# A two-layer decoder trunk on one core: the high part of x's first piece in two operations, and the squares for its row sums begun behind the second piece

## Chip, core and metric

The kernel runs on one core of a Trainium2 chip. The metric is the device time of one execution in microseconds (us); the median of several runs is given, with the lowest and the highest.

## What is computed

Two layers, each a row norm, one wide projection, four head groups and an output projection that is added to x. Cut to what the change touches:

```python
def rmsnorm(x, g):
    y = x * lax.rsqrt(jnp.mean(x * x, axis=-1, keepdims=True) + EPS)
    return y * g

def hybrid_layer(x, positions, norm_g, w_in, ..., w_out):      # x: (1, 512, 1024) float32
    h = rmsnorm(x, norm_g)
    p = h @ w_in                                               # (1024, 3488)
    (cq, ckv, kr, g_a, c_h, c_b, c_c, g_b, sg_u, sg_v, g_c, mq, mk, mv, g_d) = jnp.split(p, offs, axis=-1)
    q = rmsnorm(cq, mla_q_norm_g) @ mla_w_uq                   # low-rank q and kv
    kv = rmsnorm(ckv, mla_kv_norm_g) @ mla_w_ukv
    # (A) latent attention, (B) gated short convolution, (C) spatial gating, (D) block-sparse attention
    ...
    return jnp.concatenate([o_a * silu(g_a), o_b * silu(g_b), o_c * silu(g_c), o_d * silu(g_d)]) @ w_out

for l in range(2):
    x = x + hybrid_layer(x, ...)
```

## The kernel before

**Split products.** TensorE (PE) takes the operands of the products in the type fp32r. To keep more of float32 than that, every operand is split into a high part, the value rounded, and a low part, the rest, and every product is made of three: high by high, high by low, low by high. The high parts are written by ScalarE (ACT) or VectorE (DVE), the low parts by DVE, which reads the high part and the source. In the names h or hi stands for a high part and l or lo for a low one: hTh and hTl are the parts of x transposed, whi_ and wlo_ those of a weight unit, cTh and cTl those of cq and ckv transposed, yTh and yTl those of the first three sq units (they are kept in a buffer that later holds the heads' outputs).

**The start of layer 0.** x is (512 tokens, 1024). It arrives as pieces of 128 columns: piece k, 0 to 7, is transposed on PE into one PSUM bank (the tile xT, 128 columns of x by 512 tokens, `x_transpose`), then `x_parts` writes its high part on ACT, with the norm's gain as the scale, and its low part on DVE. Layer 0 does not divide by the row norm before the product. It multiplies by the unnormed x and puts the factor in later, so the product can start before the row sums are known. `c_first` makes the first products, cq (416 columns, in four blocks of 128 tokens): for each of the first six pieces the order on PE is four products of the high parts, the four transposes of the next piece, four with the weight's low part, four with x's low part. The weights of this product come as four units c0 to c3, each with two pieces' rows; c0's two halves land one after the other.

**The row sums.** `x_stats` squares x on ACT, 16 operations of 128 x 256 (four token blocks in each of four pairs of pieces, tile junk with the sums in xsum), each with an accumulator that is read after it. When a pair is done and transposed, its slot (one of four, x_0 .. in the rows) is released and serves others, the raw data of the units sq2 and sq3 among them, which the SP queue loads in a fixed order (`load_units`). When all are done, DVE adds the sums (TENSOR_REDUCE xv and three small TENSOR_SCALAR xv) and sets the event `v_ev`. The norms of cq and ckv (`low_stats`: ssq, e, ms) wait for it, since the factor left out changes their epsilon; ms is raised to the power -0.5 on GpSimd (POOL), and then scales the values Vt and the rotary key krt. POOL makes the rotary tables (rope_scratch) in the same stretch.

**After cq.** `low_chain` copies each token block of cq (ct), transposes it (cT), splits it (cTh, cTl) and makes q and kv from it with the units uq and ukv; the products of the token weights sq, for the spatial gate and the block-sparse queries, are interleaved.

**What sets the order.** Nothing is scheduled by hand. The class `Order` holds a clock for PE (`now`) and one for each other engine, and a list of generators with priorities. Each generator, a `Chain`, issues an instruction when its own time `t` is no more than 300 ns ahead of `now`; the clocks go forward by cost formulas in `Chain.act`, `dve`, `pool` and `pe`. An engine executes its instructions in the order in which they were issued in this way. A weight unit's high part goes to ACT or to DVE by which of the two clocks is behind (`split_units`), so an operation that is issued elsewhere can change the engine of another, and the order of all that follows. While PE has nothing to do in the first 15 us, filler products (tile warm) are issued.

Lines: all operations that go through a `Chain` have line 179 on ACT, DVE and POOL and line 209 on PE; most DMA issues of the SP queue have line 296. `x_parts` begins at line 760, `x_stats` at line 773.

Of the kernel before, what the change touches and what calls it, by code (L numbers as in the profile page):

```python
# [14 lines left out]
AF = mybir.ActivationFunctionType  # L15
# [3 lines left out]
P = 128  # L19
S = 512  # L20
# [201 lines left out]
def hybrid_trunk(ctx: ExitStack, tc: tile.TileContext, x, positions, norm_g, w_c, w_f, w_t, w_o, mla_q_norm_g,  # L222
# [3 lines left out]
    V, A, G, PE = nc.vector, nc.scalar, nc.gpsimd, nc.tensor  # L226
# [16 lines left out]
    o = Order()  # L243
# [479 lines left out]
    def pow_rstd(ch, dst, src, n):  # L723
        return ch.pow(G.tensor_tensor, dst, src, nhalf[:, :n], op=ALU.pow)
# [5 lines left out]
    xhi, xlo = ([Event() for _ in range(KT)] for _ in range(2))  # L730
# [18 lines left out]
    def x_transpose(k):  # L749

        ch = Chain(o)
        tp = yield from trS.get(ch, f"xT{k}")
        yield from ch.wait(xk_ev[k])
        for t in range(NT):
            yield from ch.pe(109.0, PE.transpose, tp[:, t * P:(t + 1) * P],
                             xk[k // 2][:, t, (k % 2) * P:(k % 2 + 1) * P], ident)
        o.set(xk_tr[k], ch.t)
        o.spawn(x_parts(k, tp, ch.t), None, -8)

    def x_parts(k, tp, t0):  # L760
        L, ch = layers[0], Chain(o, t0)
        if k // 4 not in L.h:
            L.h[k // 4] = [big.tile([P, 4, S], F32R, tag=f"h{x}{k // 4}", name=f"hT{x}{k // 4}_0") for x in "hl"]
        hi, lo = hk(L, k)
        g = gcol[:, k:k + 1]
        yield from ch.act(A.activation, hi, tp, AF.Copy, scale=g)
        o.set(xhi[k], ch.t)
        yield from ch.dve(V.scalar_tensor_tensor, lo, in0=tp, scalar=g, in1=hi.bitcast(F32),
                          op0=ALU.mult, op1=ALU.subtract)
        o.set(xlo[k], ch.t)  # L770
        trS.put(ch)

    def x_stats():
        ch = Chain(o)
        for kp in range(KT // 2):
            yield from ch.wait(xk_ev[2 * kp + 1])
            for t in range(NT):
                yield from ch.act(A.activation, junk[:, 0:2 * P], xk[kp][:, t, :], AF.Square, scale=D ** -0.5,
                                  accum_out=xsum[:, t, kp:kp + 1])
            c2 = Chain(o, ch.t)  # L780
            yield from c2.wait(xk_tr[2 * kp + 1])
            v4S.put(c2)
        yield from ch.dve(V.tensor_reduce, xv[:, RV, :], xsum, axis=AX.X, op=ALU.add)
        yield from ch.dve(V.tensor_scalar, xv[:, RV, :], xv[:, RV, :], 1.0, EPS, op0=ALU.mult, op1=ALU.add)
        t0 = ch.t
        for i, f in ((RE, EPS), (REE, EPS * EPS)):
            yield from ch.dve(V.tensor_scalar, xv[:, i, :], xv[:, RV, :], f, None, op0=ALU.mult)
        o.set(v_ev, ch.t)
        c2 = Chain(o, max(t0, ROWT))
        yield from pow_rstd(c2, xv[:, RR, :], xv[:, RV, :], NT)  # L790

        yield from c2.dve(V.tensor_copy, xr2[:, 0, :], xv[:, RR, :])
        yield from c2.dve(V.tensor_tensor, xr2[:, 1, :], xv[:, RR, :], xr2[:, 0, :].bitcast(F32), op=ALU.subtract)
        o.set(r_ev, c2.t)
# [118 lines left out]
    def hk(L, k):  # L913
        hi, lo = L.h[k // 4]
        return hi[:, k % 4, :], lo[:, k % 4, :]
# [1152 lines left out]
    def start():  # L2068
# [38 lines left out]
        o.spawn(split_units(4, len(order)), None, 5)  # L2107
        o.spawn(rope_tables(), 3700.0, 4)
        o.spawn(x_stats(), None, 5)
        o.spawn(x_row(), ROWT, 5)  # L2110
        o.spawn(main(), None, 10)
# [53 lines left out]
```

## Time and profile before

| | |
|---|---|
| three runs | 485.35, 485.96 and 486.68 us; median 485.96 |
| the profiled execution | 485.9 us, its span in the profile 484.2 us |
| granted clock of TensorE | 1.00 of full speed |
| instructions | 7554 |
| DMA | 94.21 MB in 41760 packets, mean 195 GB/s |

The profile is one execution. Times in it count from the start of its span; a row of a timeline has start, duration, engine, line, operation, the tile written, the tiles read, shapes, and in brackets how long the engine had been idle before and what released it. PEld is TensorE's loading of the stationary operand, which runs beside its products. An ACT operation's row is longer than the distance to the next one's start, since they overlap; an operation with an accumulator is followed by a row that reads it.

### The profile page before, as it was taken

To read this page: it belongs to the slowest core of one execution; us is meant where nothing else is said; L and a number is where in the kernel's file an instruction comes from. 1 tells how busy PE (TensorE), PEld (TensorE's weight loads), DVE (VectorE), ACT (ScalarE), POOL (GpSimd) and SP (SyncE) were. 2 spreads that over 40 slices of the span, in tenths; PEclk is the share of its full clock that TensorE was granted. 3 is DMA by queue.
4 is the path that set the end of the run, shared out by engine and by line. 5 is a ranking of instruction groups with operands and counts; after the bars stand their busy time and mean duration, and the time that the engine had idled before them with its cause. 6 is when DMAs were issued, how large, how long until landed. Compare 5 with 4: busy or idle time off the path is not lost. (4 is left out here: it accounts for less than half of the span.)

```text
span 484.2 us, 7554 instructions
## 1 busy us (share of the span) xinstructions
PE 478.2 (99%) x2418; PEld 406.6 (84%) x2418; DVE 399.4 (82%) x883; ACT 335.0 (69%) x895; POOL 115.2 (24%) x187
## 2 busy tenths in 40 slices
PE   8999999999999999999999999999999999999996
PEld 7988888888888888888899888888888888888785
DVE  3698877978798997779898679997788998888992
ACT  5897757776568674457577788788686888676640
POOL 8858713310421052000031004262102200000000
PEclk9999999999999999999999999999999999999999
DMA  8823076996698798685663277987824852248762
GB/s 265 306 87 110 12 229 242 235 232 168 184 282 190 219 270 260 233 283 178 214 238 131 86 268 244 263 176 226 185 87 144 161 156 106 104 158 276 271 216 87
DMA packets 41760, 94.21 MB, mean 195 GB/s; under 512 B 6114, under 2 KB 22328, under 8 KB 41336
## 3 DMA queue, kind: packets, MB, share of 16 engines
q1 hardware_dynamic: 28400, 80.74, 48.2%
q0 software_dynamic: 13216, 12.91, 17.6%
q8 instruction: 19, 0.31, 0.3%
q14 instruction: 21, 0.17, 0.1%
q10 hardware_dynamic: 104, 0.07, 0.1%
HBM read 85.58 MB, written 33.29 MB: 246 GB/s over the span
## 5 line engine op out<-in xcount | busy, mean ns | idle before, releaser
L179 ACT ACTIVATE pd<-pd,mnd 128x128 f32<-128x128 f32 (+3 forms) x53 | 27.2, 541 | 3.7 <-DVE mnd L179 3.5
L179 ACT ACTIVATE pa<-pa,mna 128x128 f32<-128x128 f32 (+3 forms) x55 | 28.1, 539 | 1.8 <-DVE mna L179 1.6
L375 POOL DMA_DIRECT2D t<-in_w_o_dram x16 | 18.6, 1323 | 30.5 <-DMA t<-t 30.4
L179 ACT ACTIVATE pha<-pTa 128x512 fp32r<-128x512 f32 (+3 forms) x32 | 13.8, 436 | 15.1 <-PE pTa L209 14.5
L179 ACT ACTIVATE phd<-pTd 128x512 fp32r<-128x512 f32 (+3 forms) x32 | 13.7, 433 | 13.0 <-PE pTd L209 12.8
L209 PE MATMUL cq<-whi_c,hTh 128*128 128x416 f32 x64 | 20.6, 367 | 0.4 <-ACT hTh L179 0.3
L179 DVE TENSOR_TENSOR pla<-pTa,pha 128x512 fp32r<-128x512 f32 (+3 forms) x32 | 15.1, 485 | 7.1 <-ACT pha L179 7.0
L179 ACT ACTIVATE whi_t<-raw_t 128x512 fp32r<-128x512 f32 x32 | 18.5, 618 | 3.3 <-DMA raw_t<-t 3.3
L179 DVE CUSTOM_DVE_ANT_0 pa<-sa,maskb,rs_q 128x512 f32<-128x512 f32 (+3 forms) x32 | 16.6, 545 | 4.8 <-PE pTa L209 2.7
L179 DVE TENSOR_TENSOR wlo_t<-raw_t,whi_t 128x512 fp32r<-128x512 f32 x32 | 20.6, 680 | 0.0
L209 PE MATMUL cq<-wlo_c,hTh 128*128 128x416 f32 x64 | 20.0, 358 | 0.0
L209 PE MATMUL cq<-whi_c,hTl 128*128 128x416 f32 x64 | 19.8, 356 | 0.0
L179 DVE TENSOR_TENSOR wlo_p<-raw_p,whi_p 128x512 fp32r<-128x512 f32 x28 | 18.9, 698 | 0.7 <-ACT whi_p L179 0.6
L179 DVE TENSOR_TENSOR pld<-pTd,phd 128x512 fp32r<-128x512 f32 (+3 forms) x32 | 15.1, 486 | 4.6 <-ACT phd L179 4.3
L179 DVE CUSTOM_DVE_ANT_0 pd<-sd,maskb,rs_mq 128x512 f32<-128x512 f32 (+3 forms) x32 | 16.7, 545 | 1.6 <-PE pTd L209 0.8
L179 ACT ACTIVATE whi_b<-raw_b 128x512 fp32r<-128x512 f32 x23 | 13.8, 621 | 4.1 <-DMA raw_b<-in_w_o_dram 4.0
L179 DVE TENSOR_TENSOR wlo_b<-raw_b,whi_b 128x512 fp32r<-128x512 f32 x24 | 16.1, 683 | 0.1
L179 ACT ACTIVATE whi_p<-raw_p 128x512 fp32r<-128x512 f32 x26 | 15.6, 625 | 0.7 <-DMA raw_p<-p 0.7
L179 POOL TENSOR_TENSOR rs_mk<-rs_mk,nhalf 128x16 f32<-128x16 f32 x2 | 5.9, 2926 | 42.5 <-ACT gc L179 21.5
L179 POOL TENSOR_SCALAR xss<-xss 128x1 f32<-128x1 f32 x4 | 2.7, 669 | 54.6 <-ACT jk L179 50.2
L375 POOL DMA_DIRECT2D p<-in_w_t_dram x8 | 9.8, 1486 | 23.0 <-DMA p<-p 11.8
L209 PE MATMUL pTa<-ident,pa 128*128 128x128 f32 x80 | 14.0, 273 | 0.0
(499 smaller groups left out, 1854.4 us busy)
## 6 DMA issues: line engine op xcount, KB each, us to landing
t<-in_w_o_dram POOLq DMA_DIRECT2D x16, 512.0 KB, 8.6
raw_t<-t SPq DMA_DIRECT2D x16, 512.0 KB, 4.9
raw_b<-in_w_o_dram SPq DMA_DIRECT2D x12, 512.0 KB, 5.0
t<-in_w_o_dram SPq DMA_DIRECT2D x8, 512.0 KB, 5.3
p<-in_w_t_dram POOLq DMA_DIRECT2D x8, 512.0 KB, 12.4
t<-t SPq DMA_DIRECT2D x8, 512.0 KB, 4.9
raw_p<-p SPq DMA_DIRECT2D x8, 512.0 KB, 4.7
ys<-ysc SPq DMA_DIRECT2D x14, 256.0 KB, 5.6
```

Source lines behind the costliest of these rows:

```text
L179: f(*a, **k)
L209: f(*a, **k)
L375: nc.gpsimd.dma_start(src(l, n, j), src(l, y, j), accum_op=ALU.add, max_dma_last_dim=1024)
```

## The change

The high part of piece 0 is written by two ACT operations, of tokens 0 to 255 and 256 to 511, and the planner's event for it is set by the first of them. The other seven pieces are left as they were. The chain that issues the squares starts with the time 8600 ns where it started with the planner's clock at that moment, so its first square is issued later among ACT's instructions.

```diff
         g = gcol[:, k:k + 1]
-        yield from ch.act(A.activation, hi, tp, AF.Copy, scale=g)
-        o.set(xhi[k], ch.t)
+        n = 2 * P if k == 0 else S
+        yield from ch.act(A.activation, hi[:, 0:n], tp[:, 0:n], AF.Copy, scale=g)
+        t1 = ch.t
+        if n < S:
+            yield from ch.act(A.activation, hi[:, n:S], tp[:, n:S], AF.Copy, scale=g)
+        o.set(xhi[k], t1)
         yield from ch.dve(V.scalar_tensor_tensor, lo, in0=tp, scalar=g, in1=hi.bitcast(F32),
                           op0=ALU.mult, op1=ALU.subtract)
         o.set(xlo[k], ch.t)
         trS.put(ch)
 
     def x_stats():
-        ch = Chain(o)
+        ch = Chain(o, 8600.0)
         for kp in range(KT // 2):
             yield from ch.wait(xk_ev[2 * kp + 1])
             for t in range(NT):
```

The number of squares, of products for the result and of bytes moved stays as it is. Since the order of everything behind these two places is worked out anew by the planner, it differs on all engines in layer 0; PE's differs up to its row 916 of 2271 in the program's order, and is the same from there on. One filler product at the start is gone, and two of the high part's operations stand where one stood.

## The prediction

> **What bounds the kernel now.** I read the profile from the whole to the place: first the page's busy times, then TensorE's (PE's) busy time by stretches of the span, then the waits of PE, then the timelines of the first 30 us, engine by engine. The page's first part, and two stretches and the sum from the table of busy time by windows (length, then busy time of PE, PEld, DVE, ACT and POOL, then granted clock, DMA share and GB/s):
>
> ```profile
> PE 478.2 (99%) x2418; PEld 406.6 (84%) x2418; DVE 399.4 (82%) x883; ACT 335.0 (69%) x895; POOL 115.2 (24%) x187
> ...
> 0.00:5.70 5.70, 4.16 (x21) 3.68 (x21) 1.44 (x5) 2.15 (x3) 3.84 (x44) 1.00 0.62 166
> 5.70:20.00 14.30, 14.12 (x81) 12.99 (x81) 8.44 (x14) 12.02 (x39) 12.48 (x30) 1.00 1.04 376
> 20.00:40.00 20.00, 20.00 (x107) 17.74 (x107) 18.29 (x47) 18.03 (x62) 13.40 (x23) 1.00 0.29 84
> ...
> 460.00:484.20 24.20, 20.32 (x101) 17.09 (x99) 15.34 (x27) 5.19 (x10) 0.00 (x0) 1.00 0.45 151
> sum 484.20, PE 478.17 PEld 406.57 DVE 399.36 ACT 335.01 POOL 115.15; mean PE 36.78 PEld 31.27 DVE 30.72 ACT 25.77 POOL 8.86
> ```
>
> PE is idle for 484.20 - 478.17 = 6.0 us in all: 5.70 - 4.16 = 1.5 us before its first real product, 0.2 us in the next 14, 24.20 - 20.32 = 3.9 us behind its last work, and 0.4 us in the 440 us between. So PE's in-order stream sets the time. An edit gains only what it takes from the idle time at the start, and loses whatever it makes PE wait later. In the same 20 us that follow the start, DVE (18.29 of 20.00) and ACT (18.03) are nearly full as well: work that is pushed into that stretch has little cover. PE's timeline at the start (start, duration, instructions of four each; a merged row's duration includes the tail of its last product):
>
> ```profile
> 5.77 1.02 PE L209 MATMUL cq<-whi_c,hTh 128*128 128x416 f32 x4 [0.33 <-ACT hTh L179]
> ...
> 7.82 0.92 PE L209 MATMUL cq<-whi_c,hTl 128*128 128x416 f32 x4
> 8.84 1.02 PE L209 MATMUL cq<-whi_c,hTh 128*128 128x416 f32 x4
> ...
> 10.89 0.92 PE L209 MATMUL cq<-whi_c,hTl 128*128 128x416 f32 x4
> 11.65 0.99 PE L209 MATMUL cq<-whi_c,hTh 128*128 128x416 f32 x4
> ...
> 29.25 0.45 PE L209 MATMUL q<-whi_uq,cTl 128*128 128x384 f32 x1
> ```
>
> Four products without a wait take 11.65 - 10.89 = 0.76 us. PE was therefore free for piece 1 at 7.82 + 0.76 = 8.58 and began at 8.84: 0.26 us of waiting that the page's tails hide. ACT's timeline beside it:
>
> ```profile
> 5.03 0.69 ACT L179 ACTIVATE hTh<-xT,pg 128x512 fp32r<-128x512 f32 x1 [1.81 <-PE xT L209]
> ...
> 7.26 0.55 ACT L179 ACTIVATE whi_c<-raw_c 128x416 fp32r<-128x416 f32 x1 [0.94 <-DMA raw_c<-in_w_c_dram]
> 7.72 0.40 ACT L179 ACTIVATE junk<-x 128x256 f32<-128x256 f32 x1
> ...
> 8.12 0.67 ACT L179 ACTIVATE hTh<-xT,pg 128x512 fp32r<-128x512 f32 x1
> ...
> 10.04 0.55 ACT L179 ACTIVATE whi_c<-raw_c 128x416 fp32r<-128x416 f32 x1 [0.31 <-DMA raw_c<-in_w_c_dram]
> 10.49 0.40 ACT L179 ACTIVATE junk<-x 128x256 f32<-128x256 f32 x1
> ...
> 10.89 0.67 ACT L179 ACTIVATE hTh<-xT,pg 128x512 fp32r<-128x512 f32 x1
> ...
> 32.18 0.48 ACT L179 ACTIVATE Q<-q 128x384 f32<-128x384 f32 x1
> ...
> 33.21 0.36 ACT L179 ACTIVATE K<-kv 128x256 f32<-128x256 f32 x1
> ```
>
> **Part 1, the first piece in two operations.** 128 columns less cost 0.48 - 0.36 = 0.12 us from PSUM, so a half of 256 takes 0.69 - 2 x 0.12 = 0.45 us and ends at 5.48; the product followed the whole one by 5.77 - 5.72 = 0.05, so it starts at 5.53, 0.24 us earlier. The second half ends near 5.9, when the two products of the first half (0.38 us) are just done. The low part on DVE, which reads both halves, is 0.15 to 0.2 us later and still a product group ahead of its reader. The dropped filler product costs nothing: it only filled idle time.
>
> **Part 2, the squares behind piece 1.** ACT's order at the start, before (hTh is the high part of a piece of x, junk,xsum a square):
>
> ```order
> L179 ACTIVATE hTh_0_230<-xT_224,pg 128x512
> L179 ACTIVATE junk,xsum<-x_0_174 128x256
> L179 ACTIVATE whi_c_0_199<-raw_c_0_201 128x416
> L179 ACTIVATE junk,xsum<-x_0_174 128x256
> L179 ACTIVATE hTh_0_230<-xT_243,pg 128x512
> L179 ACTIVATE junk,xsum<-x_0_174 128x256 x2
> L179 ACTIVATE whi_c_0_245<-raw_c_0_206 128x416
> L179 ACTIVATE junk,xsum<-x_0_175 128x256
> L179 ACTIVATE hTh_0_230<-xT_271,pg 128x512
> ```
>
> and now:
>
> ```order
> L179 ACTIVATE hTh_0_230<-xT_224,pg 128x256 x2
> L179 ACTIVATE whi_c_0_199<-raw_c_0_201 128x416
> L179 ACTIVATE hTh_0_230<-xT_241,pg 128x512
> L179 ACTIVATE whi_c_0_244<-raw_c_0_206 128x416
> L179 ACTIVATE junk,xsum<-x_0_174 128x256
> L179 ACTIVATE hTh_0_230<-xT_267,pg 128x512
> ```
>
> Four squares left the place ahead of the second weight unit; one still stands between that unit's high part and piece 2. Piece 1's high part starts at 7.72 instead of 8.12, so its product could start at 8.44 instead of 8.84: 0.40 us ahead. But the next weight unit lands when it did (the 10.04 row waits for its DMA), and behind it come the same square and the same hTh: piece 2 is ready at 10.89 + 0.67 + 0.05 = 11.61, against 11.65 before. Of the 0.40 us, 0.04 is kept; between 0 and 0.1 with the ends of these rows. From there to 24.4 us ACT's order is the old one, with the squares' inputs shifted by four.
>
> The four squares return at 25 to 33 us, in the full stretch. Each takes 0.40 us there or 0.53 ahead of another that writes junk, 1.6 to 2.1 us together. ACT alone would still have cTh ready for PE, but the order also hands one high part of a weight unit from ACT to DVE. DVE's order ahead of cTl, the low part that PE reads at 29.25, before (yTh and whi_sq are weight units, ct a copy of cq):
>
> ```order
> L179 SCALAR_TENSOR_TENSOR hTl_0_375<-xT_445,pg,hTh_0_374 128x512
> L179 TENSOR_REDUCE xv<-xsum 128x4
> L179 SCALAR_TENSOR_TENSOR wlo_uq_219<-raw_uq_214,pcol,whi_uq_218 128x384
> L179 TENSOR_SCALAR xv<-xv 128x4
> L179 COPY ct_0_489<-cq_0_220 128x416
> L179 TENSOR_SCALAR xv<-xv 128x4
> L179 COPY ct_0_499<-cq_0_221 128x416
> L179 TENSOR_SCALAR xv<-xv 128x4
> L179 SCALAR_TENSOR_TENSOR wlo_ukv_450<-raw_ukv_216,pcol,whi_ukv_449 128x256
> L179 CAST whi_sq_0_526<-raw_sq_0_338 128x512
> L179 COPY ct_0_532<-cq_0_222 128x416
> L179 TENSOR_TENSOR cTl_0_512<-cT_0_491,cTh_0_511 128x384
> ```
>
> and now:
>
> ```order
> L179 SCALAR_TENSOR_TENSOR hTl_0_355<-xT_440,pg,hTh_0_354 128x512
> L179 SCALAR_TENSOR_TENSOR wlo_uq_219<-raw_uq_214,pcol,whi_uq_218 128x384
> L179 SCALAR_TENSOR_TENSOR wlo_ukv_446<-raw_ukv_216,pcol,whi_ukv_445 128x256
> L179 COPY ct_0_485<-cq_0_220 128x416
> L179 COPY ct_0_494<-cq_0_221 128x416
> L179 SCALAR_TENSOR_TENSOR wlo_ukv_446<-raw_ukv_216,pcol,whi_ukv_445 128x256
> L179 CAST yTh<-raw_sq_0_332 128x512
> L179 CAST whi_sq_0_520<-raw_sq_0_387 128x512
> L179 COPY ct_0_526<-cq_0_222 128x416
> L179 TENSOR_TENSOR cTl_0_507<-cT_0_487,cTh_0_506 128x384
> ```
>
> Four small xv operations leave, since the sums they need come later; a second wlo_ukv and a CAST move in. DVE's and POOL's rows of before for these:
>
> ```profile
> 24.84 0.16 DVE L179 TENSOR_REDUCE xv<-xsum 128x4 f32<-128x16 f32 x1
> 24.91 0.61 DVE L179 SCALAR_TENSOR_TENSOR wlo_uq<-raw_uq,pcol,whi_uq 128x384 fp32r<-128x384 f32 x1
> 25.44 0.43 DVE L179 TENSOR_SCALAR xv<-xv 128x4 f32<-128x4 f32 x1
> 25.78 0.58 DVE L179 COPY ct<-cq 128x416 f32<-128x416 f32 x1
> ...
> 26.92 0.70 DVE L179 SCALAR_TENSOR_TENSOR wlo_ukv<-raw_ukv,pcol,whi_ukv 128x256 fp32r<-128x256 f32 x1
> 27.55 0.68 DVE L179 CAST whi_sq<-raw_sq 128x512 fp32r<-128x512 f32 x1
> 28.15 0.58 DVE L179 COPY ct<-cq 128x416 f32<-128x416 f32 x1
> 28.65 0.54 DVE L179 TENSOR_TENSOR cTl<-cT,cTh 128x384 fp32r<-128x384 f32 x1
> 29.11 0.47 DVE L179 SCALAR_TENSOR_TENSOR wlo_ukv<-raw_ukv,pcol,whi_ukv 128x256 fp32r<-128x256 f32 x1
> 29.51 1.28 DVE L179 TENSOR_TENSOR yTl<-raw_sq,yTh 128x512 fp32r<-128x512 f32 x2
> ...
> 35.24 1.55 DVE L179 TENSOR_TENSOR wlo_sq<-raw_sq,whi_sq 128x512 fp32r<-128x512 f32 x2
> ```
>
> From start to start, the first xv takes 24.91 - 24.84 = 0.07 us and the second 25.78 - 25.44 = 0.34; the other two by the smaller figure, 0.14. So 0.55 leaves, 29.51 - 29.11 = 0.40 to 27.55 - 26.92 = 0.63 comes for wlo_ukv and 28.15 - 27.55 = 0.60 for the CAST. DVE reaches cTl later by 0.45 to 0.68 us. PE was already held by it (28.65 + 0.54 + 0.05 against 29.25), so PE waits one for one. If the second xv would have been as short as the others and the CAST half as long, 0.2 is the lower end; if both wlo_ukv take the long price, 0.8. I take 0.5. This replaces the 0.04 of part 2, which is earlier on the same stream.
>
> **What else moves.** The slots of x serve as buffers of the last two sq units. The fourth and eighth squares release them; they now stand where the eighth and the twelfth stood:
>
> ```profile
> 14.26 1.28 SPq L296 DMA_DIRECT2D raw_sq<-in_w_t_dram  x2
> ...
> 19.11 0.41 ACT L179 ACTIVATE junk<-x 128x256 f32<-128x256 f32 x1
> ```
>
> The second of these loads is issued near 19.7 instead of 15.2, and lg_b, the other small loads and cw stand behind it on SP's queue. The DMA section gives 7.0 us from issue to landing for these units:
>
> ```profile
> raw_sq<-in_w_t_dram SPq DMA_DIRECT2D x4, 512.0 KB, 7.0
> ```
>
> It lands at 26.7, and its first reader on DVE, the CAST whi_sq, stands near 28: hidden, with 1 us to spare. If that is gone, DVE and PE wait one for one. POOL's order of this time, before (ms is a row norm, rope_scratch the rotary tables):
>
> ```order
> L179 TENSOR_TENSOR rope_scratch<-rope_scratch,ones 128x128
> L179 TENSOR_TENSOR ms_0_550<-ms_0_550,nhalf 128x2
> L179 TENSOR_TENSOR ms_0_567<-ms_0_567,nhalf 128x2
> L179 TENSOR_TENSOR rope_scratch<-rope_scratch 128x128
> L179 TENSOR_TENSOR ms_0_618<-ms_0_618,nhalf 128x2
> L179 TENSOR_TENSOR rope_scratch<-rope_scratch,ones 128x128
> ```
>
> and now:
>
> ```order
> L179 TENSOR_TENSOR rope_scratch<-rope_scratch,ones 128x128
> L179 TENSOR_TENSOR rope_scratch<-rope_scratch 128x128
> L179 TENSOR_TENSOR rope_scratch<-rope_scratch,ones 128x128
> L179 TENSOR_TENSOR rope_scratch<-rope_scratch 128x128
> L179 TENSOR_TENSOR rope_scratch<-rope_scratch,ones 128x64
> L179 TENSOR_TENSOR rope_scratch<-rope_scratch 128x64
> L179 TENSOR_SCALAR rope_scratch<-rope_scratch 128x64
> L179 TENSOR_TENSOR ms_0_560<-ms_0_560,nhalf 128x2
> ```
>
> Before, POOL stood still ahead of the first ms:
>
> ```profile
> 28.02 0.47 POOL L179 TENSOR_TENSOR rope_scratch<-rope_scratch,ones 128x128 f32<-128x128 f32 x1
> 33.88 0.73 POOL L179 TENSOR_TENSOR ms<-ms,nhalf 128x2 f32<-128x2 f32 x1 [5.39 <-DVE ms L179]
> ```
>
> Now six rope operations fill that gap, beside DVE's six yTl subtractions. wlo_ukv took 0.70 beside rope and 0.47 when POOL stood still, 0.23 more. The next low part that PE needs, cTl of the second token block, stands behind those six. From the start of the first cTl, PE reaches it after 0.59 us of that cTl itself, 9 products of 0.17 to 0.23 us, 12 of 0.23 and a transpose, together 5.3; DVE after 0.46 + 6 x 0.60 + 0.59 = 4.65. So there is 0.7 us of slack. The surcharge lies between nothing and 0.47 a piece (the whole length of the last rope row), 2.8 in all; I take half of 6 x 0.23, by the nearest row and since POOL stands still for part of the time: 0.7, just hidden. [...]
>
> After about 215 us PE's order is the same as before; in between, layer 0's attention steps and weight splits stand in other places among the same products. PE waits for 0.4 us in all of that now, so little can be gained and something lost; I put it at 0, with 0.5 either way.
>
> **The sum.** The profiled execution took 485.9 us, its span 484.2, so 1.7 lie outside; the median of three is 485.96, the same within 0.1. 485.9 + 0.5 = 486.4.
>
> **The rivals.** Forecast: the head start is pinned by the DMA at piece 2, and DVE is 0.5 us late once: 486.4; chance 0.55.
> Gain kept: cTl is not later (CAST and wlo_ukv at their short prices, POOL out of the way) and piece 2 comes 0.4 earlier: 485.5. Against it stands the DMA behind the 10.04 row. 0.15.
> Slow: DVE becomes the bound from 29 to 36 us, through rope. At cTl of the second block the six subtractions are late by their surcharge less 0.7, so it decides from 0.7 on and makes the kernel measurably slower from 1.7 on. At 6 x 0.35, midway between 0.23 and 0.47, it is 2.1, PE waits 1.4, and the time is 485.9 + 0.5 + 1.4 = 487.8. For it: 26.92. Against it: the pair at 35.24, beside one rope operation, paid 1.55 - 1.28 = 0.27 for both. 0.22.
> Faster: the reshuffled layer 0 loses its waits and the head start stays whole: 0.24 + 0.26 + 0.4 = 0.9, 485.0; to be measurably faster more would have to go than PE waits. 0.08 for what I don't see.
>
> **The numbers.** 0.3% is 1.5 us, about what a measurement of this kernel can tell from no change. Forecast and kept gain lie within it, with part of the slow case's lower end: same 0.73; slower 0.20; faster 0.07. The range reaches from the faster case (485.0, less 0.1) to the slow one (487.8) plus 0.3 for a second wait of the same kind: 484.9 to 488.1.
>
> **What would show it.** Right: the first product near 5.53, the product of piece 1 near 8.44, that of piece 2 at 11.6; the first q<-whi_uq,cTl near 29.7, with the releaser DVE cTl. Wrong: piece 2 at 11.3 (gain kept), yTl rows of 0.8 us and a second wait for cTl before 36 us (slow), a CAST whi_sq behind its DMA, or waits of over 0.5 us between 60 and 215 us.

## The result, and the profile after

The changed kernel takes 490.05 us (median of 6 runs, 487.81 to 490.68) against 485.60 (6 runs): a ratio of 1.0082, 95% interval 1.0065 to 1.0098. It is slower by some 4 us, where 486.4 within 484.9 to 488.1 was forecast.

The profiled execution of after took 489.97 us with a span of 488.2, 4.0 more than before's. Its busy times by stretches (columns as in the table of before):

```profile
0.00:5.70 5.70, 4.56 (x19) 4.06 (x19) 1.45 (x5) 1.85 (x3) 4.65 (x45) 1.00 0.55 163
5.70:20.00 14.30, 13.75 (x80) 12.96 (x80) 8.19 (x13) 10.41 (x31) 12.31 (x31) 1.00 1.00 359
20.00:40.00 20.00, 19.50 (x105) 17.14 (x104) 17.60 (x45) 17.99 (x65) 10.77 (x23) 1.00 0.32 97
...
150.00:160.00 10.00, 8.80 (x49) 7.10 (x47) 6.04 (x16) 5.68 (x14) 0.00 (x0) 1.00 0.78 186
...
190.00:200.00 10.00, 8.01 (x40) 6.22 (x38) 5.28 (x11) 3.76 (x8) 2.63 (x4) 1.00 0.88 263
```

PE is idle in two new places: 10 - 8.80 = 1.2 us behind 150 us and 10 - 8.01 = 2.0 behind 190, in the stretch in which before lost 0.4 in all. The waits of PE name who ended them (total, times, longest):

```profile
PE od L209 <- ACT phd L179: 1.9, 1, 1.9
PE sd L209 <- DVE mnd L179: 1.2, 1, 1.2
PE warm L2083 <- DVE ones L2080: 1.1, 1, 1.1
PE cq L209 <- ACT hTh L179: 0.6, 2, 0.4
PE q L209 <- DVE cTl L179: 0.5, 1, 0.5
PE ox L209 <- DVE wlo_t L179: 0.2, 1, 0.2
```

sd and od are products of layer 0's block-sparse attention (D); phd is the high part of the transposed weights pd. On PE's timeline:

```profile
154.21 0.39 PE L209 MATMUL cb<-hTh,wlo_cb 128*128 128x512 f32 x1
155.80 0.33 PE L209 MATMUL sd<-mk1d,mq1d 128*128 128x128 f32 x1 [1.20 <-DVE mnd L179]
...
195.18 0.40 PE L209 MATMUL gb<-hTh,wlo_gb 128*128 128x512 f32 x1
197.49 0.39 PE L209 MATMUL od<-phd,Mt 128*128 128x256 f32 x1 [1.92 <-ACT phd L179]
```

The idle time in brackets leaves out the tail of the product ahead. From start to start sd comes 1.59 us behind that product and od 2.31, where the products before them follow each other every 0.23 us; so the two places cost some 1.4 and 2.1 us.

The releaser did not cause the wait. First DVE's timeline ahead of the sd product at 155.80, whose PSUM bank is freed by the mask operation at 155.26:

```profile
151.11 0.69 DVE L179 TENSOR_TENSOR th_gd<-gd,rh 128x512 f32<-128x512 f32 x1 [0.47 <-PE gd L209]
154.32 0.43 DVE L179 CAST whi_cc<-raw_cc 128x512 fp32r<-128x512 f32 x1 [2.52 <-DMA raw_cc<-in_w_f_dram]
154.66 0.68 DVE L179 SCALAR_TENSOR_TENSOR th_gd<-gd,th_gd 128x512 f32<-128x512 f32 x1
155.26 0.47 DVE L179 CUSTOM_DVE_ANT_0 pd<-sd,maskb,rs_mq 128x256 f32<-128x256 f32 x1
```

then ACT's ahead of the od product at 197.49:

```profile
190.99 0.49 ACT L179 ACTIVATE phd<-pTd 128x384 fp32r<-128x384 f32 x1 [0.43 <-PE pTd L209]
196.54 0.63 ACT L179 ACTIVATE whi_b<-raw_b 128x512 fp32r<-128x512 f32 x1 [5.05 <-DMA raw_b<-in_w_o_dram]
197.07 0.53 ACT L179 ACTIVATE phd<-pTd 128x256 fp32r<-128x256 f32 x2
```

In both, the high part of a weight unit (cc1; b110) is next on an engine that works in order, and its load has not landed: DVE stands for 2.52 us and ACT for 5.05, with the attention's step behind it, which was ready before the load landed. In before neither waited for its load:

```profile
155.36 0.62 ACT L179 ACTIVATE whi_cc<-raw_cc 128x512 fp32r<-128x512 f32 x1
...
191.35 1.14 ACT L179 ACTIVATE whi_b<-raw_b 128x512 fp32r<-128x512 f32 x2
```

The start, on PE and ACT:

```profile
5.86 1.02 PE L209 MATMUL cq<-whi_c,hTh 128*128 128x416 f32 x4 [0.18 <-ACT hTh L179]
...
8.67 0.92 PE L209 MATMUL cq<-whi_c,hTh 128*128 128x416 f32 x4
...
11.92 0.83 PE L209 MATMUL cq<-whi_c,hTh 128*128 128x416 f32 x3 [0.39 <-ACT hTh L179]
...
30.10 0.44 PE L209 MATMUL q<-whi_uq,cTl 128*128 128x384 f32 x1 [0.49 <-DVE cTl L179]
```

```profile
5.33 0.84 ACT L179 ACTIVATE hTh<-xT,pg 128x256 fp32r<-128x256 f32 x2 [2.11 <-PE xT L209]
...
10.34 0.56 ACT L179 ACTIVATE whi_c<-raw_c 128x416 fp32r<-128x416 f32 x1 [2.29 <-DMA raw_c<-in_w_c_dram]
```

PE is 0.85 us later than before at the first q<-whi_uq,cTl (30.10 against 29.25). With the 1.2 and the 2.0 that is 4.05, about the difference of the spans. Counted at places where both kernels have done the same products, after is 0.8 us behind before at 60 us, 2.2 at 183, 4.3 at 200 and 4.0 at the end.

### The profile page after: what moved, and what is told of

It reads as the page before. It is cut to its first block, busy times and chain, and to the rows that moved or that the text cites. A ratio compares the mean times of both kernels' runs of the same rounds, so it can differ in the third digit from the quotient of the medians.

```text
span 488.2 us, 7567 instructions
## 1 busy us (share of the span) xinstructions
PE 478.8 (98%) x2416; PEld 406.8 (83%) x2416; DVE 397.9 (82%) x884; ACT 335.6 (69%) x913; POOL 116.7 (24%) x187
## 4 chain that ended last, share of the span: by engine, by line
PE 84%; DVE 7%; DMA 6%; SPq 1%; ACT 1%; issue 1%; DVEq 0%; ACTq 0%
PE oy L209 6%; PE kv L209 6%; PE cq L209 5%; PE su L209 5%; PE ch L209 5%; PE sq L209 4%; PE ga L209 4%; PE cc L209 4%; PE gb L209 4%; PE gc L209 4%; PE py L209 3%; PE ox L209 3%; PE sa L209 3%; PE cb L209 3%; PE gd L209 2%; PE pz L209 2%
## 5 line engine op out<-in xcount | busy, mean ns | idle before, releaser
L179 ACT ACTIVATE pd<-pd,mnd 128x384 f32<-128x384 f32 (+3 forms) x54 | 27.8, 541 | 3.5 <-DVE mnd L179 3.2
L179 ACT ACTIVATE pa<-pa,mna 128x256 f32<-128x256 f32 (+3 forms) x50 | 25.9, 540 | 0.6 <-DVE mna L179 0.5
```

Of the source, the lines that this page charges most:

```text
L179: f(*a, **k)
```

## The experiments

**Theory (order).** The edit itself costs the half microsecond of the sum. The rest is the planner's: it deals layer 0 out anew, and weight splits that wait for their loads come to stand ahead of attention steps that PE waits for. **Rivals:** the squares' late place makes the whole loss at the start; the two physical halves cost; the loads are late, wherever their readers stand. Every ratio is to the kernel before, run beside it on the same chip, with its 95% interval.

**One instruction moved.** On the changed kernel:

```diff
-    LATE = {"ch1_0": 2500.0, "p220_1": 3000.0}
+    LATE = {"ch1_0": 2500.0, "p220_1": 3000.0, "b110_0": 4000.0}
```

> The changed kernel with one ACT instruction moved: the first high part of weight unit b110, which waited 5.05 us for its load, stands behind the last two phd of layer 0 instead of ahead of them; no other instruction of any engine moves. Order theory (the loss is made where a weight split that waits for its load stands ahead of attention steps that PE waits for): the 1.9 us wait of PE's od product on phd near 197 us goes, and the time is 490.05 - 1.9 = 488.1, between 487.8 and 488.5. If the loss is made at the start, by the squares' late place on ACT or by DVE's cTl, or by the physical halves: no change, 489.6 to 490.5. If the loads themselves are late and not the order: the wait only moves to the products that read unit b110, and the time stays over 489.5.

Measured: 489.20 us (6 runs, 487.80 to 493.43), 1.0084 (1.0052 to 1.0117). The wait of 1.9 is gone from the list of PE's waits, and nothing took its place:

```profile
PE sd L209 <- DVE mnd L179: 1.2, 1, 1.2
PE warm L2083 <- DVE ones L2080: 1.1, 1, 1.1
PE q L209 <- DVE cTl L179: 0.3, 1, 0.3
```

So the load was not too late for its own reader, which speaks against the last rival. ACT still waits for the loads of raw_b, 5.8 us in all where after has 9.9, but no wait of PE comes of it. The median fell by 0.9 only, not 1.9, and lies above what was expected; with six scattered runs the ratio tells this kernel from the changed one no better than from the forecast. In the profiled run the gain can be read: PE's rows, in the same order in both, are 1.0 us later than in after ahead of the od product and 1.5 us earlier behind it, 2.5 us by one instruction. That run (487.89) started badly: PE ran at half rate for longer (last section).

**Both splits planned later.** `"b110_0": 5000.0, "cc1_0": 3000.0` in the same table.

> The changed kernel with both weight splits planned later (units cc1 by 3.0 us and b110 by 5.0 us in the table of late loads); 108 of PE's rows move against the changed kernel, all behind 150 us, so the start is the changed kernel's own. Order theory: the waits of 1.2 us near 155.8 and 1.9 us near 197.5 both go and nothing takes their place: 490.05 - 1.2 - 1.9 = 486.9, between 486.4 and 487.6. If the loss is made at the start or by the physical halves: 489.6 to 490.5. If the loads are late and not the order: over 489, with the waits at other products.

Measured: 485.95 us, 1.0007 (0.9995 to 1.0019), below what was expected, which had counted the two waits by their idle time alone. Both waits are gone, and the start is the changed kernel's:

```profile
PE warm L2083 <- DVE ones L2080: 1.1, 1, 1.1
PE q L209 <- DVE cTl L179: 0.5, 1, 0.5
PE cq L209 <- ACT hTh L179: 0.3, 1, 0.3
PE oy L209 <- DVE wlo_t L179: 0.2, 1, 0.2
```

The late squares and the halves are both still there, and the loss is not: the first two rivals fall as causes of the 4 us.

**Either part alone.** First the halves, then the squares:

```diff
-        yield from ch.act(A.activation, hi, tp, AF.Copy, scale=g)
+        n = 2 * P if k == 0 else S
+        yield from ch.act(A.activation, hi[:, 0:n], tp[:, 0:n], AF.Copy, scale=g)
...
```

> The kernel before with the high part of the first piece in two operations and nothing else in the text; the planner moves 314 of PE's rows against before, over much of layer 0. Order theory: this edit can lose time in other places than the change does, by 0 to 3 us, as its order falls, and any loss shows as waits of PE behind 30 us on steps that stand behind a split waiting for its load; the start itself gives up to 0.25 us. Theory that the start makes the loss by the squares in the full stretch from 25 to 33 us: no squares are moved here, so 485.3 to 485.9. Theory that the physical halves cost: about the changed kernel's 490.

```diff
-        ch = Chain(o)
+        ch = Chain(o, 8600.0)
```

> The kernel before with only the squares begun behind the second piece's high part, the first piece's high part whole. The splits of cc1 and b110 stand on ACT and DVE where the changed kernel has them, ahead of the same attention steps. Order theory: the same two waits near 155 and 197 us, 489.5 to 490.5. Theory that the squares' late place makes the loss at the start: also about 490, but with no waits of over 0.5 us between 100 and 215 us and with PE late by 3 us or more before 40 us. Theory that the physical halves cost: 485.5 to 486.5.

Measured: the halves 485.66 us, 1.0006 (0.9994 to 1.0019), and no wait of PE over 0.4 us behind 30 us: another order need not cost anything. The squares 489.35 us, 1.0094 (1.0057 to 1.0131). The time is 0.15 us under what was expected, and the places fit only in part. Its waits of PE:

```profile
PE sd L209 <- DVE mnd L179: 2.6, 1, 2.6
...
PE pTd L209 <- ACT pd L179: 1.1, 1, 1.1
```

SP issues the load of cc1, and DVE's split waits for it:

```profile
147.92 0.33 SPq L296 DMA_DIRECT2D raw_cc<-in_w_f_dram  x1
...
155.41 0.43 DVE L179 CAST whi_cc<-raw_cc 128x512 fp32r<-128x512 f32 x1 [3.96 <-DMA raw_cc<-in_w_f_dram]
```

155.41 - 147.92 = 7.5 us from issue to use. In after the issue stands at 148.25 and the use at 154.32, 6.1 us. The extra 1.4 us are PE's, one for one: 2.6 against 1.2. The wait for od did not come, since b110 landed in time here. The 1.1 for pTd is another unit's: on ACT the split of gc1 waits 2.08 us for its load at 189.19, ahead of the pd that PE needs. So the order decides which load PE is exposed to, and the load's own time what that costs.

**Three instructions moved.** The changed kernel's plan, with the issue of named splits held back by so many instructions of their engine:

```diff
     def _emit(self, e, cost, f, a, k):
...
+        n = self.hold.get(e, 0)
+        if n:
+            self.o.held.append([e, n, lambda: f(*a, **k)])
+            return
         f(*a, **k)
+        for h in [h for h in self.o.held if h[0] == e]:
+            h[1] -= 1
+            if h[1] == 0:
+                self.o.held.remove(h)
+                h[2]()
...
+                if u.name == "cc1_0":
+                    c2.hold = {"V": 5, "A": 2}
```

with `"b110_0": 4000.0` as above.

> The changed kernel with three instructions moved and no other: the two high parts of weight unit cc1 that waited for its load (one on DVE, one on ACT) are issued behind five and two of the next steps of their engine, and the first high part of unit b110 behind the last two phd. PE's, POOL's and SP's orders are the changed kernel's, row by row. Order theory: both waits of PE go (1.2 to 2.6 us near 155, 1.9 near 197), and the time is 490.05 - 1.2 - 1.9 = 486.9, between 485.8 and 487.6. If something else in the changed order makes the loss (PE's own order, the place of the loads on SP, the late squares, the halves): 489.0 to 490.5.

Measured: 487.05 us, 1.0027 (1.0014 to 1.0039). Three of the 7567 instructions take 3.0 of the 4.45 us (2.7 of 4.0 by the ratios). One wait is new in the list:

```profile
PE pTd L219 <- ACT pd L184: 0.9, 1, 0.9
```

and ACT's timeline has the same picture again, at unit gc1:

```profile
187.76 0.63 ACT L184 ACTIVATE whi_gc<-raw_gc 128x512 fp32r<-128x512 f32 x1 [1.92 <-DMA raw_gc<-in_w_f_dram]
188.30 1.91 ACT L184 ACTIVATE pd<-pd,mnd 128x512 f32<-128x512 f32 x4
```

In after ACT waits at this place too, for 0.77 us, which PE's slack hid:

```profile
186.77 0.63 ACT L179 ACTIVATE whi_gc<-raw_gc 128x512 fp32r<-128x512 f32 x1 [0.77 <-DMA raw_gc<-in_w_f_dram]
```

From issue to use the load took 186.77 - 181.09 = 5.7 us there and 187.76 - 180.93 = 6.8 here, with SP's, POOL's and PE's orders the same. The order holds more such exposures than one execution shows.

**Four instructions moved.** As above, and

```diff
+                if u.name == "gc1_0" and i == 0:
+                    c2.hold = {"A": 4}
```

> As the run with three moved instructions, and the first high part of unit gc1 issued behind the four normalizations of pd, ahead of which it waited for its load. Order theory: the wait of 0.9 us near 190 us goes as well: 487.05 - 0.9 = 486.1, between 485.6 and 486.7, about the blind sum of 486.4. If the rest of the loss is the edited start's: no change, 486.8 to 487.3.

Measured: 486.16 us, 1.0000 (0.9988 to 1.0013). With those four instructions elsewhere and all else as in the changed kernel, PE's row by row order included, the loss is gone: nothing by the ratio, with 0.6 us either way, in which the 0.5 us of the sum lies too. In this run's profile PE is 1.1 us behind before at 60 us, 0.65 at 200, and 0.14 ahead at the end, each time where both have done the same products. So the start does lose, more than the sum had, and what follows wins it back, the last 0.8 us where PE's order is the same in both; the sum had neither. That 486.16 lies near the forecast 486.4 is in part luck.

**Other start times of the squares.** 9600.0 and 7600.0 instead of 8600.0:

> The changed kernel with the squares begun at 9.6 us of the planner's time instead of 8.6: nearly the same squares in the same places at the start, another order in layer 0 (422 of PE's rows differ from the changed kernel's). Order theory: the time is another throw of the same dice, anywhere from 485.5 to 490.5, and what it is over 486.4 stands in the waits of PE behind 30 us. Theory that the squares' late place makes the loss: 489.5 to 490.5, with no such waits.

> As the run with 9.6 us, with the squares begun at 7.6 us: again another order (836 of PE's rows differ from the changed kernel's). Order theory: anywhere from 485.5 to 490.5 or somewhat more, with the excess over 486.4 in the waits of PE behind 30 us. Theory that the squares' late place makes the loss: 489.5 to 490.5 without such waits.

Measured: 487.15 us, 1.0029 (1.0015 to 1.0042), and 492.78 us, 1.0142 (1.0119 to 1.0164). The second is outside what was expected, on the slow side, and its waits are in yet other places: 2.2 us at oy in the output projection and 1.3 at cc.

The first's profiled run was its fastest (485.33) and has no wait of PE over 0.5 us behind 30 us, so where its median loses 1.5 us stays open.

**Nudges of the plan alone.** The kernel before, with one number more in the table of late loads (`"ga0_0": 1500.0`; then kv0, su0, gc0):

> The kernel before with one entry more in the planner's table of late loads (unit ga0 of layer 0 by 1.5 us) and no operation added, removed or made longer: the first 273 of PE's rows stay, 292 differ behind them. If the planner's order of layer 0 is by itself worth some us: between 485.0 and 490, and at least one of the four nudges over 486.6 or under 484.6, its excess in waits of PE behind 35 us. If only the edited start makes a loss: 485.2 to 486.0, all four.

> As the run with ga0, with unit kv0 of layer 0 by 1.5 us: 316 of PE's rows differ, from row 220 on. The same numbers by each theory.

> As the run with ga0, with unit su0 of layer 0 by 1.5 us: 300 of PE's rows differ, from row 389 on. The same numbers by each theory.

> As the run with ga0, with unit gc0 of layer 0 by 1.5 us: 286 of PE's rows differ, from row 402 on. The same numbers by each theory.

Measured: ga0 486.18 us, 1.0013 (0.9999 to 1.0027); kv0 487.68, 1.0040 (1.0021 to 1.0059); su0 485.25, 0.9990 (0.9977 to 1.0003); gc0 487.53, 1.0047 (1.0026 to 1.0069). Two of four lose 2 us with no edit of the work at all. The worst waits of kv0's and gc0's runs, 1.3 and 1.6 us, are the change's own, at the same sd product behind the split of cc1. In gc0's:

```profile
154.55 0.43 DVE L179 CAST whi_cc<-raw_cc 128x512 fp32r<-128x512 f32 x1 [2.95 <-DMA raw_cc<-in_w_f_dram]
```

**The halves without the planner.** The kernel before, with two operations in the one step that the planner reckons:

```diff
+        def halves(out, in_, f, **kw):
+            for z in (slice(0, 2 * P), slice(2 * P, S)) if k == 0 else (slice(0, S),):
+                A.activation(out[:, z], in_[:, z], f, **kw)
-        yield from ch.act(A.activation, hi, tp, AF.Copy, scale=g)
+        yield from ch.act(halves, hi, tp, AF.Copy, scale=g)
```

> The kernel before with the first piece's high part issued as two operations while the planner reckons with one, so that the orders of PE, ACT, POOL and SP are those of before but for the two halves. The prediction's price of part 1 alone: the first product 0.24 us earlier, of which piece 2, pinned by its load, keeps little: 485.5, between 485.2 and 485.7. If the physical halves cost: over 486.

Measured: 485.39 us, 0.9993 (0.9982 to 1.0003): 0.2 us less by the medians, which these runs can't tell from nothing, nor from the 0.24 us of the prediction's price. The same edit on the su0 nudge:

> The kernel before with unit su0 entered 1.5 us late in the planner's table (which gave 485.25) and the first piece's high part in two operations that the planner reckons as one. Order theory and the price of part 1: 485.25 - 0.2 = 485.0, between 484.6 and 485.4, a ratio of about 0.9987. If the two small gains were chance: 485.4 to 485.8.

Measured: 485.20 us, 0.9983 (0.9972 to 0.9993): the one version that is faster than the kernel before by more than its interval, by some 0.8 us. How much of it is the order and how much the halves, these runs don't separate.

## Why the prediction was wrong, by its steps

**What bounds the kernel.** Right: PE's in-order stream, 0.4 us idle in 440. But where little can be gained, the next question is how much can be lost.

**Part 1.** Right in size, not in the place. From the start of the high part to the product it is 5.77 - 5.03 = 0.74 us in before and 5.86 - 5.33 = 0.53 in after, 0.21 less where 0.24 was forecast. With the halves alone the product starts at 5.50 (5.53 forecast). In after it starts at 5.86, because the transposes ahead of it ran at half rate: 1.11 us for four, against 0.65 in before.

**Part 2.** Right. Piece 1's product came without a wait, and piece 2 was pinned by its weight unit. The forecast 11.61 became 11.92 since the unit landed at 10.34 instead of 10.04. Across eleven of the executions it was used between 9.67 and 10.67, without any edit that concerns it.

**DVE and cTl.** Right: q<-whi_uq,cTl with the releaser DVE cTl, 0.85 us later, of which 0.27 came with piece 2 (11.92 against 11.65), so 0.58 of its own; 0.5 was taken. The wait itself is 0.49, and 0.5 in five more runs that have the squares late. DVE's rows show the two that moved in, and behind cTl the six subtractions:

```profile
27.23 0.70 DVE L179 SCALAR_TENSOR_TENSOR wlo_ukv<-raw_ukv,pcol,whi_ukv 128x256 fp32r<-128x256 f32 x1
27.85 0.62 DVE L179 CAST yTh<-raw_sq 128x512 fp32r<-128x512 f32 x1
28.40 0.68 DVE L179 CAST whi_sq<-raw_sq 128x512 fp32r<-128x512 f32 x1
...
29.50 0.54 DVE L179 TENSOR_TENSOR cTl<-cT,cTh 128x384 fp32r<-128x384 f32 x1
29.97 3.69 DVE L179 TENSOR_TENSOR yTl<-raw_sq,yTh 128x512 fp32r<-128x512 f32 x6
```

**The sq load and POOL.** Right on the load: the CAST whi_sq has no wait. Wrong on the overlap, which did not come in after. POOL's last rope operation of this stretch ends at 29.71 + 0.38 = 30.09, and POOL then stands still until 37.80:

```profile
29.71 0.38 POOL L179 TENSOR_SCALAR rope_scratch<-rope_scratch 128x64 f32<-128x64 f32 x1
```

So the six subtractions at 29.97 ran almost by themselves, and that they paid no surcharge there (0.60 us from start to start) says nothing of the price. In other runs with the squares late POOL had more to do in this stretch: from 20 to 32 us it was busy for 10.03 us with both splits planned later and for 10.36 with the squares alone, against 8.57 in after, and the six took 3.95 us in both. The first of the two:

```profile
29.29 3.95 DVE L179 TENSOR_TENSOR yTl<-raw_sq,yTh 128x512 fp32r<-128x512 f32 x6
```

With 9600 five of them took 3.39 us, where after's first five took 3.08. So the surcharge, if all of it is POOL's, is 0.26 us for six and 0.31 for five, some 0.05 a piece, where 0.7 was taken for the six. That a piece pays up to 0.47 (the top of the range), or 0.35 (the slow rival), was the author's estimate, and no run shows it. No run has a second wait of PE for cTl, so it was hidden, and the slow rival, with 2.1 for the six, is out.

**The step that failed:** "PE waits for 0.4 us in all of that now, so little can be gained and something lost; I put it at 0, with 0.5 either way." The reshuffled stretch from 60 to 215 us cost 3.2 us in the profiled run by the idle time of its two waits, 4.3 - 0.8 = 3.5 by PE's lateness, and about 3.9 by the four moves (490.05 - 486.16; 4.0 by the ratios). A count of the idle time says what an order can give, not what another can take. The bound should have come from the splits in that stretch: each waits for a load, which in after took 5.7 us from issue to use for gc1, 6.1 for cc1 and 9.7 for b110 (issued at 186.86, used at 196.54), and whichever the new order puts ahead of a step that PE needs can cost what is left of it. The order told which ones: one half of whi_cc had gone from ACT to DVE, ahead of a mask operation, and whi_b stood ahead of two phd. The nudges' medians, -0.4 to +2.0 us, give the price that belonged into the range. The sign for being wrong, "waits of over 0.5 us between 60 and 215 us", was the one that came.

## What to carry to other kernels

Where a planner orders the instructions, an edit is two edits: what it does, and the new order that follows. Measure the second by itself, with nudges of the plan that change no work, and measure the first with the plan held. On in-order engines, look in the new order for every instruction that waits for a load and has a step of the critical stream behind it, the hidden waits too: a load that lands a microsecond later in another execution exposes them.

## What the runs showed of the hardware

**PE's first microseconds run at half rate, for a time that differs between executions, and the column of the granted clock doesn't show it.** The same products in the run with one instruction moved, where PE's order is that of after:

```profile
5.86 1.76 PE L209 MATMUL cq<-whi_c,hTh 128*128 128x416 f32 x4
7.42 1.05 PE L209 MATMUL xT<-ident,x 128*128 128x128 f32 x4
```

1.76 us where after has 1.02, at a granted clock of 1.00 in both. By the distance of starts (0.21 us for 128 columns, then 0.11) the full rate begins at 4.3 us or earlier in before and 5.3 to 5.9 in after. In that run and in the one with three instructions moved the half rate lasts beyond 8.1, where one product of cq<-wlo_c takes 0.69 us in both, against 0.35 later on; PE had been at work since 1.1 us in all. It left those two 1.1 and 1.3 us later than after at 30 us (the first q<-whi_uq,cTl at 31.16 and 31.39, against 30.10), and so is part of the scatter of a kernel's runs. In before, in after and in six more of the runs the first four products take 1.02 or 1.03 us, from 5.50 to 6.08 on. What ends the half rate, and what delayed that in the two, stays open.

**The same load of 512 KB takes up to 1.6 us more or less from one execution to the next, with SP's order the same:** from issue to use gc1's took 5.2 us with one instruction moved (182.10 to 187.30), 5.7 in after and 6.8 with three moved, and ACT stood waiting for it in all three. What slows it was not separated.
